# Weight casts moved to later rounds, x loaded first, and the second block's gates ahead of the first up projection, in a hybrid decoder layer on eight cores

## The chip, the cores and the metric

The kernel runs on the 8 cores of one Trainium2 chip. Each core computes one element of a batch of 8, and the cores exchange nothing. The metric is device time in microseconds (us) of the slowest core. Most executions of one kernel agree within 0.3%. In some executions the cores of one die, or of both, show a lower granted TensorE clock (0.80 to 0.95 instead of about 0.97) and the time is longer. Such slow runs are in no comparison below.

## The reference, cut to what matters

```python
# x: (8, 4096, 1024) f32; D = 1024, one layer
z = h @ w_in                        # -> q | k | v (768 each), u (512), g (2048)
# B: dilated causal window attention, 3 groups (window, dilation) x 4 heads of 64,
#    the groups mixed by their softmax denominators -> y_attn (4096, 256)
# A: s5_ssm(u): 32 groups of 16 channels, 64 complex states, a scan over 4096 steps
y_ssm = gelu(s5_ssm(u, ...)); a, b = split(y_ssm @ w_glu); y_ssm = a * sigmoid(b)
gate_ssm, gate_attn = split(sigmoid(g + b_gate))
mix = (gate_ssm * (y_ssm @ w_ssm_proj) + gate_attn * (y_attn @ w_attn_proj)) @ w_out
h = layer_norm(ALPHA * h + mix)
ff = square(relu(h @ w_up)) @ w_down           # 1024 -> 4096 -> 1024
h = layer_norm(ALPHA * h + ff)
```

## The kernel before

Every operation is recorded with the resources that it reads and writes. A list scheduler (I call it the planner) with constant cost estimates then fixes the order of every engine's instructions. The engines run these orders strictly in sequence and wait on semaphores. The planner's times are no times of the chip.

The stages of one core:

1. Load x and the first weights; U, the state-space layer's input projection (TensorE); "prep", its tables (VectorE, GpSimd).
2. Six rounds (three dilations, two head pairs). Each computes q, k and v of its heads and then attends. The state-space layer's 32 groups run in between.
3. Eight blocks of 512 tokens: gates g (GLU, gates, branch projections), o (output projection, first layer norm), up, d (down, second layer norm). Block b's gates are computed after up of block b-1, and its o inside d of block b-1.

Weights lie in DRAM as f32. Matmuls read bf16 copies (`wb_*`) made by casting transfers, here called casts. In rounds 1 and 2 there are 18 casts, 16 of 512 KB and two (`wb_ap`) of 256 KB, counted in bytes written; up and down are cast on the way to SBUF in block 0 (`first`) and stored from there for the later blocks.

```python
# loads at the start
dma("pool", wu[0].ap, wu_d[0], [], [wu[0]])
for s in range(8):
    dma("pool", xT.ap[:, :, s * 512:(s + 1) * 512], xT_d[s], [], [xT.res[s]])
    if s == 0:
        ...                                  # the other wu, then wq of round 0
...
dma("sp", smI.ap, smI_d, [], [smI])          # tables of the state-space layer
dma("sp", smB.ap, smB_d, [], [smB])

# U: two buffers us, stored to u_d
for fp in range(2):
    for s in range(8):
        for ft in (2 * fp, 2 * fp + 1):
            ub = us[ft % 2]
            ...                              # 8 matmuls
            cp("act", ub.ap[:, :, s * 32:(s + 1) * 32], ..., [bk], [ub])
    for ft in (2 * fp, 2 * fp + 1):
        dma("sp", u_d[ft], us[ft % 2].ap, [us[ft % 2]], [u_res.res[ft]])

# casts: a list of closures; each reads `pace`, the resource that it waits for
wcast.append(lambda pace, c=c_: dma("pool", dst[i, c], src[i, c]..., pace, [...]))
for name in ("glu", "gate", "sp", "ap", "out"):
    ...
# inside the rounds, after the copy of q or k (of v likewise)
cp("act", o, i, [bk], wr)
if rnd > 0 and t % 2 == 1 and wcast:
    wcast.pop(0)(wr[:1])       # the cast "reads" a part of qT or kT

# state-space layer: two store buffers
ysg = ysb[g % 2]
cp("act", ysg.ap, bk.ap..., [bk], [ysg])
for t in range(2):
    dma("act", y_d[g, :, t * 8:t * 8 + 8]..., ysg.ap[:, t, :], [ysg], [...])

# blocks: a ring of eight 1-MB slots for weights
def load_piece(name, i, first=False):
    slot = min((r for r in ring if id(r) not in live), key=last_use)
    if first:                                # cast into the slot, store bf16 for later
        dma("pool", slot.ap[:, 0:sz], src[i]..., [], [slot])
        dma("sp", dst[i], slot.ap[:, 0:sz], [slot], ...)
    else:
        dma("sp", slot.ap[:, 0:sz], dst[i], ..., [slot])

stage_g(0); ...                              # then stage_o of block 0
for blk in range(NB):
    stage_up(blk)                            # load_piece("up", up, blk == 0)
    if nxt:
        stage_g(blk + 1)
    pcs = [load_piece("dn", q, blk == 0) for q in range(4)]
    ...                                      # stage_d, with stage_o of the next block
```

The softmax here doesn't subtract the row's maximum and nothing guards it: scores larger than these inputs give would overflow.

## Time and profile before

The time is 2053.69 us (median of 6 runs, 2050.78 to 2062.69). The slowest core of the profiled run is core 3, and lines below without another core are of core 3.

From the page: the span, and three of the rows of 40 slices of about 51 us. A digit is the share of a slice in tenths that TensorE was busy, the granted TensorE clock, or the share that the core's 16 DMA engines were busy.

```profile
span 2049.2 us, 31367 instructions; the slowest of 8 cores (2035.1 to 2049.2 us)
...
PE   2898876999977697999999999999999999999996
...
PEclk8999988999998898999999999999999999999998
DMA  9946887551179949974565547366456543734531
```

Counting slices from 1, TensorE is full from slice 17 on; the change can only win before. The DMA row there shows 8, 8 and 7 in slices 5 to 7 (rounds 1 and 2, with the casts), 1 1 in slices 10 and 11 (rounds 4 and 5) and 9 9 in slices 13 and 14 (block 0). That is the invitation of this change: DMA work crowds where TensorE has gaps, and hardly any runs in rounds 4 and 5, where TensorE is full.

Waits of before (engine and line, what it waited for: us in total, times, longest):

```profile
ACT arena L497 <- DMA y_scratch<-arena: 16.8, 3, 11.4
...
ACT arena L497 <- DMA wb_out<-w_out: 16.0, 2, 9.4
...
PE ps L451 <- DMA arena<-wb_out: 9.3, 1, 9.3
...
PE ps L451 <- DMA arena<-w_down: 7.4, 1, 7.4
...
ACT arena L497 <- DMA wb_ap<-w_attn_proj: 5.7, 1, 5.7
```

The second and fifth line are the casts: ScalarE (ACT) copies into a part of qT, kT or V which a cast still "reads" as its pace token, and so waits until the cast has landed. This read is a fiction of the bookkeeping. The first line is different: the state-space output waits for a free store buffer, hence for a store that is slow in landing.

### The profile page before, as it was taken

What the parts mean: (1) busy time and instruction counts of PE and PEld (TensorE: products, weight loads), DVE (VectorE), ACT (ScalarE), POOL (GpSimd) and SP (SyncE); (2) the same over time, 40 slices, a digit from 0 to 9 for tenths busy, and PEclk for the clock granted to TensorE, in tenths of its full rate; (3) what the DMA queues carried; (4) which work ended last, traced back from release to release, by engine and by line L of the source; (5) the groups of instructions that cost most, each with busy time, mean ns of one, the idle gap of its engine ahead of it and who ended that gap; (6) DMA issues with size and microseconds to landing.
All of it is one profiled execution on the core that took longest, in us unless ns stands there. A gap on an engine that the chain in (4) does not pass through costs nothing.

```text
span 2049.2 us, 31367 instructions; the slowest of 8 cores (2035.1 to 2049.2 us)
## 1 busy us (share of the span) xinstructions
PE 1872.7 (91%) x10468; PEld 923.6 (45%) x10468; DVE 959.1 (47%) x1396; ACT 695.8 (34%) x1053; POOL 295.7 (14%) x322
## 2 busy tenths in 40 slices
PE   2898876999977697999999999999999999999996
PEld 1454453665643343444444444444444444444442
DVE  6944542763344431553553354256355336535524
ACT  2446432655564341224213213412421331232120
POOL 5743212120003002000100200100010020010000
PEclk8999988999998898999999999999999999999998
DMA  9946887551179949974565547366456543734531
GB/s 173 213 149 208 176 163 177 146 149 42 32 229 224 242 142 200 265 269 144 170 245 177 170 150 251 124 229 234 131 166 231 192 165 139 252 139 146 220 107 41
DMA packets 110189, 359.72 MB, mean 176 GB/s; under 512 B 10288, under 2 KB 55728, under 8 KB 81328
## 3 DMA queue, kind: packets, MB, share of 16 engines
q1 hardware_dynamic: 75872, 265.33, 37.8%
q0 software_dynamic: 25456, 83.99, 20.3%
q10 hardware_dynamic: 8704, 8.39, 1.3%
q8 instruction: 88, 1.44, 0.3%
q14 instruction: 69, 0.57, 0.1%
HBM read 339.94 MB, written 74.97 MB: 202 GB/s over the span
## 4 chain that ended last, share of the span: by engine, by line
PE 73%; DVE 7%; DMA 7%; ACT 5%; issue 5%; POOL 1%; ACTq 1%; DVEq 0%; POOLq 0%; SPq 0%
PE ps L451 72%; DVE arena L491 4%; ACT arena L497 3%; DMA y_scratch<-arena 2%; ACT arena L463 2%; DVE arena L481 2%; DMA arena<-wb_out 1%; PE ps L456 1%; DMA wb_out<-w_out 1%; DMA arena<-x_tile 1%; ACT L463 1%; ACTq L441 1%; DVE arena L1084 1%; DMA tab_scratch<-arena 1%; POOL arena L481 0%
## 5 line engine op out<-in xcount | busy, mean ns | idle before, releaser
L451 PE MATMUL ps<-arena 128*128 128x512 bf16 (+4 forms) x10148 | 1854.7, 344 | 118.8 <-ACT arena L497 29.1
L451 PEld LDWEIGHTS ps<-arena 128*128 128x128 bf16 (+2 forms) x10148 | 908.5, 104 | 1046.0 <-issue 208.9
L463 ACT ACTIVATE arena<-ps 128x512 f32<-128x512 f32 (+2 forms) x384 | 261.2, 680 | 388.5 <-PE ps L451 301.9
L491 DVE SCALAR_TENSOR_TENSOR arena<-ps,arena 128x512 bf16<-128x512 f32 x256 | 176.8, 691 | 245.6 <-ACT arena L463 245.6
L481 DVE TENSOR_TENSOR arena<-arena 128x512 f32<-128x512 f32 (+7 forms) x267 | 195.3, 756 | 177.6 <-ACT arena L463 164.5
L481 POOL TENSOR_TENSOR arena<-arena 128x512 bf16<-128x512 f32 (+1 forms) x128 | 165.3, 1294 | 766.1 <-DVE arena L481 633.6
L481 DVE TENSOR_TENSOR arena<-ps,arena 128x512 f32<-128x512 f32 (+1 forms) x193 | 127.5, 687 | 290.4 <-PE ps L451 237.8
L463 ACT ACTIVATE arena<-arena 128x512 f32<-128x512 f32 (+6 forms) x186 | 101.5, 548 | 292.4 <-DVE arena L1086 256.8
L491 DVE SCALAR_TENSOR_TENSOR arena<-arena,ps 128x512 f32<-128x512 f32 x128 | 87.1, 686 | 228.3 <-PE ps L451 227.1
L497 ACT CAST arena<-ps 128x512 bf16<-128x512 f32 (+1 forms) x217 | 122.1, 569 | 180.9 <-PE ps L451 120.7
L491 DVE SCALAR_TENSOR_TENSOR arena<-arena 128x1024 f32<-128x1024 f32 (+1 forms) x131 | 167.1, 1276 | 21.2 <-ACT arena L463 6.5
L463 ACT ACTIVATE arena<-ps,arena 128x512 f32<-128x512 f32 x128 | 86.0, 687 | 165.6 <-POOL arena L481 138.7
L441 POOL DMA_DIRECT2D out<-arena x32 | 17.3, 541 | 597.8 <-DVE arena L491 597.8
L463 ACT ACT_TABLE_LOAD x42 | 53.9, 1283 | 143.7 <-DVE arena L1086 125.6
L1084 DVE BATCH_NORM_STATS2 arena<-arena 128x6 f32<-128x512 f32 x128 | 88.8, 694 | 12.2
L456 PE MATMUL ps<-arena 128*128 128x128 bf16 (+1 forms) x320 | 39.6, 243 | 40.7 <-ACT arena L497 21.4
L497 ACT COPY arena<-ps 128x512 f32<-128x512 f32 (+1 forms) x64 | 51.2, 799 | 65.1 <-PE ps L456 27.2
L497 ACT CAST arena<-arena 128x1024 bf16<-128x1024 f32 x32 | 33.5, 1046 | 103.2 <-DVE arena L491 103.2
L456 PEld LDWEIGHTS ps<-arena 128*128 128x128 bf16 (+1 forms) x320 | 29.1, 122 | 62.1 <-issue 61.8
L481 DVE TENSOR_TENSOR arena<-arena,ps 128x512 f32<-128x512 f32 x64 | 41.0, 681 | 7.8 <-PE ps L451 7.8
L487 POOL TENSOR_SCALAR arena<-arena 128x256 f32<-128x256 f32 x32 | 39.1, 1224 | 9.4 <-DMA tab_scratch<-arena 6.4
L488 DVE TENSOR_SCALAR arena<-arena 128x512 f32<-128x512 f32 (+2 forms) x19 | 9.5, 498 | 43.7 <-POOL arena L487 43.3
(28 smaller groups left out, 153.6 us busy)
## 6 DMA issues: line engine op xcount, KB each, us to landing
arena<-wb_up SPq DMA_DIRECT2D x56, 1024.0 KB, 9.7
arena<-wb_dn SPq DMA_DIRECT2D x56, 1024.0 KB, 4.9
arena<-wb_gate SPq DMA_DIRECT2D x32, 1024.0 KB, 6.2
arena<-wb_out SPq DMA_DIRECT2D x16, 1024.0 KB, 9.0
arena<-x POOLq DMA_DIRECT2D x32, 512.0 KB, 10.5
out<-arena POOLq DMA_DIRECT2D x32, 512.0 KB, 4.3
arena<-x_tile POOLq DMA_DIRECT2D x8, 1024.0 KB, 48.5
tab_scratch<-arena SPq DMA_DIRECT2D x16, 512.0 KB, 4.2
```

The source lines that it names most:

```text
L441: return P.add(eng, lambda e: e.dma_start(out=out, in_=in_), R(*reads), R(*writes), dma=True, nbytes=nb)
L451: return P.add("pe", lambda e: e.matmul(out, lhsT, rhs, start=start, stop=stop, **kw), R(*reads), R(*writes), cost=c)
L456: return P.add("pe", lambda e: e.transpose(out, in_, ident), R(*reads), R(*writes), cost=c)
L463: return P.add("act", lambda e: e.activation(out, in_, func, bias=bias, scale=scale), R(*reads), R(*writes), cost=c, aset=ASETS.get(func))
L481: return P.add(eng, lambda e: e.tensor_tensor(out, in0, in1, op), R(*reads), R(*writes), cost=ew_cost(eng, out, [in0, in1], True))
L487: return P.add(eng, lambda e: e.tensor_scalar(out, in0, s1, None, op0), R(*reads), R(*writes), cost=c)
L488: return P.add(eng, lambda e: e.tensor_scalar(out, in0, s1, s2, op0, op1), R(*reads), R(*writes), cost=c)
L491: return P.add("dve", lambda e: e.scalar_tensor_tensor(out, in0, scalar, in1, op0, op1), R(*reads), R(*writes), cost=160.0 + 1.06 * fsize( ...
L497: return P.add("act", lambda e: e.copy(out, in_), R(*reads), R(*writes), cost=c)
L1084: P.add("dve", (lambda hf_: lambda e: e.bn_stats(st6[:, hf_ * 6:hf_ * 6 + 6], xb.ap[:, hf_ * 512:hf_ * 512 + 512]))(hf), R(xb), R(m), cost ...
```

## The change

Its intent: take the casts out of the crowded rounds 1 and 2 and put them, with the 16 casts of the down weights, into rounds 3 to 5; give x the first DMA time; let block 0 start without waiting for the attention's buffers; fill TensorE's gaps in block 0 with block 1's gates.

```diff
-    dma("pool", wu[0].ap, ...); for s in range(8): x tile s, after tile 0 the other weights
+    for item in ("u0", 0, "u1", "q0", "q1", 1, "q2", 2, "u2", "u3", 3, 4, 5, 6, 7):
+        ...                                     # numbers are x tiles
-    dma("sp", smI.ap, smI_d, [], [smI])
+    dma("sp", smI.ap, smI_d, [xT.res[XS]], [smI])          # XS = 2; smB likewise
-    dma("pool", shf.ap, shf_d, [], [shf])
+    dma("pool", shf.ap, shf_d, [xT.res[7]], [shf])
...
-    for name in ("glu", "gate", "sp", "ap", "out"):
+    for name in ("glu", "gate", "sp", "ap", "out", "dn"):
...
+    def pace(op, rnd, t):
+        if rnd > 2 and t % 2 == 1 and wcast:
+            after = Res()
+            after.w = op                        # waits for the copy, blocks nobody
+            wcast.pop(0)([after])
-                cp("act", o, i, [bk], wr)
-                if rnd > 0 and t % 2 == 1 and wcast:
-                    wcast.pop(0)(wr[:1])
+                pace(cp("act", o, i, [bk], wr), rnd, t)      # of v likewise
...
-            dma("sp", ya_d[...], ys_.ap, ...)
+            dma("act", ya_d[...], ys_.ap, ...)
...
+    ar.seek(E0, S1)                             # the state-space layer's region
+    ring = [ar.alloc([4096], BF16)]             # first slot; then yf, xTb, yT
     ar.seek(X0, Q0)
-    ring = [ar.alloc([4096], BF16) for _ in range(8)]
+    ring += [ar.alloc([4096], BF16) for _ in range(7)]      # mixin here; lnr, hT moved too
...
+            P.at("p3", 3)                       # the output projection's add goes first
             stt(xo, xo, ALPHA, bk.ap, ALU.mult, ALU.add, [x_, bk], [x_])
...
+    load_x(1)
+    stage_g(1)
     for blk in range(NB):
         stage_up(blk)
-        if nxt:
+        if nxt and blk:
             stage_g(blk + 1)
-        pcs = [load_piece("dn", q, blk == 0) for q in range(4)]
+        pcs = [load_piece("dn", q) for q in range(4)]        # the other four likewise
```

More of the change, by code (lines that the diff above doesn't have):

```diff
@@ L24 @@
 KB = 1024
+XS = 2
 class Res:
@@ L558, in build_program @@
     P.at("U", 2)
-    dma("pool", wu[0].ap, wu_d[0], [], [wu[0]])
-    for s in range(8):
-        dma("pool", xT.ap[:, :, s * 512:(s + 1) * 512], xT_d[s], [], [xT.res[s]])
-        if s == 0:
-            for ft in range(1, 4):
-                dma("pool", wu[ft].ap, wu_d[ft], [], [wu[ft]])
-            for j in range(3):
-                dma("pool", wq[j].ap, wqkv_d[0, :, j * 8:(j + 1) * 8, :], [], [wq[j]])
+    for item in ("u0", 0, "u1", "q0", "q1", 1, "q2", 2, "u2", "u3", 3, 4, 5, 6, 7):
+        if isinstance(item, int):
+            dma("pool", xT.ap[:, :, item * 512:(item + 1) * 512], xT_d[item], [], [xT.res[item]])
+        elif item[0] == "u":
+            dma("pool", wu[int(item[1])].ap, wu_d[int(item[1])], [], [wu[int(item[1])]])
+        else:
+            j = int(item[1])
+            dma("pool", wq[j].ap, wqkv_d[0, :, j * 8:(j + 1) * 8, :], [], [wq[j]])
     n = 0
@@ L583, in build_program @@
     smI = ar.alloc([SI_N], F32)
-    dma("sp", smI.ap, smI_d, [], [smI])
+    dma("sp", smI.ap, smI_d, [xT.res[XS]], [smI])
     smB = ar.alloc([SB_N], F32)
-    dma("sp", smB.ap, smB_d, [], [smB])
+    dma("sp", smB.ap, smB_d, [xT.res[XS]], [smB])
     shf = ar.alloc([384], BF16)
-    dma("pool", shf.ap, shf_d, [], [shf])
+    dma("pool", shf.ap, shf_d, [xT.res[7]], [shf])
     gcs = [ar.alloc([2, 2, 256], F32) for _ in range(3)]
@@ L898, in build_program @@
             o = V.ap[:, t4 * 4:t4 * 4 + 4].rearrange("p b (s d) -> p b s d", d=64)[:, :, 0:3:2, :]
-            cp("act", o, bk.ap.rearrange("p (b s d) -> p b s d", b=4, s=2), [bk], [V.res[t4 * 4 + j] for j in range(4)])
-            if rnd > 0 and t4 % 2 == 1 and wcast:
-                wcast.pop(0)(V.res[t4 * 4:t4 * 4 + 1])
+            pace(cp("act", o, bk.ap.rearrange("p (b s d) -> p b s d", b=4, s=2), [bk],
+                    [V.res[t4 * 4 + j] for j in range(4)]), rnd, t4)
         if rnd < 5:
@@ L974, in norm @@
             tt("dve", ys_.ap[64:128], a1[64:128], rn.ap[64:128], ALU.mult, r1 + [rn], [ys_])
-            dma("sp", ya_d[hp, :, 2 * b:2 * b + 2, :].rearrange("p r c -> p (r c)"), ys_.ap, [ys_], [ya_res.res[hp * 8 + b]])
+            dma("act", ya_d[hp, :, 2 * b:2 * b + 2, :].rearrange("p r c -> p (r c)"), ys_.ap, [ys_], [ya_res.res[hp * 8 + b]])
         def pv(q, j, pt):
@@ L1011, in build_program @@
         c([])
-    ar.seek(X0, Q0)
-    ring = [ar.alloc([4096], BF16) for _ in range(8)]
-    ar.seek(Q0, Q1)
+    ar.seek(E0, S1)
+    ring = [ar.alloc([4096], BF16)]
+    yf = ar.alloc([4, 512], F32, nres=4)
     xTb = ar.alloc([8, 512], BF16)
     yT = ar.alloc([4, 512], BF16)
+    ar.seek(X0, Q0)
+    ring += [ar.alloc([4096], BF16) for _ in range(7)]
+    mixin = ar.alloc([8, 512], BF16, nres=8)
+    ar.seek(Q0, Q1)
     y2T = ar.alloc([4, 512], BF16, nres=4)
@@ L1020, in build_program @@
     gsb, gab = ar.alloc([512], F32), ar.alloc([512], F32)
-    ar.seek(E0, S1)
-    yf = ar.alloc([4, 512], F32, nres=4)
-    mixin = ar.alloc([8, 512], BF16, nres=8)
-    E1 = ar.off
+    lnr = [ar.alloc([D], F32) for _ in range(4)]
     ar.seek(Q1, A0)
@@ L1028, in build_program @@
     aT = ar.alloc([32, 512], BF16, nres=32)
-    ar.seek(E1)
+    ar.seek(S1)
     hT = ar.alloc([8, 512], BF16, nres=4)
-    lnr = [ar.alloc([D], F32) for _ in range(4)]
     hb = [ar.alloc([1024], BF16) for _ in range(1)]
@@ L1168, in stage_o @@
             xo = x_.ap[:, oh * 512:(oh + 1) * 512]
+            P.at("p3", 3)
             stt(xo, xo, ALPHA, bk.ap, ALU.mult, ALU.add, [x_, bk], [x_])
+            P.at("p3", 7)
         P.at("ln1", 4)
@@ L1217, in build_program @@
     done(*wo)
+    load_x(1)
+    stage_g(1)
     for blk in range(NB):
         nxt = blk + 1 < NB
-        if nxt:
+        if nxt and blk:
             load_x(blk + 1)
         stage_up(blk)
-        if nxt:
+        if nxt and blk:
             stage_g(blk + 1)
         P.at("p3", 7)
-        pcs = [load_piece("dn", q, blk == 0) for q in range(4)]
+        pcs = [load_piece("dn", q) for q in range(4)]
         if nxt:
             wo = [load_piece("out", oh) for oh in range(2)]
-        pcs2 = [load_piece("dn", 4 + q, blk == 0) for q in range(2)]
+        pcs2 = [load_piece("dn", 4 + q) for q in range(2)]
         for t in range(TB):
@@ L1237, in build_program @@
             done(*wo)
-        pcs2 += [load_piece("dn", 6 + q, blk == 0) for q in range(2)]
+        pcs2 += [load_piece("dn", 6 + q) for q in range(2)]
         for t in range(TB):
```

## The prediction

> **What bounds the kernel now.** TensorE: busy 1872.7 of 2049.2 us, 73% of the chain of waits. From 834 us on it is solid (the windows show 1177 of the last 1199 us busy; one 512-token block takes 172 us). The 176 us without a matmul lie almost all before 834 us: 48 in 0-125, 20 in 200-300, 16 in 300-350, 38 in 575-690, 18 in 690-850. Around them the granted clock falls too (0.59 in 675-700), as the Trainium skill, "TensorE: Matmul & The Clock Gate", Part 1, says of an idle array; a removed gap is worth more than its idle time.
>
> **Step 1, casts to rounds 3-5, with their own pace token.** In round 2 a cast reads part of qT or kT that a later copy writes again, so ACT waits for the cast's landing: 5.74, 6.55 and 9.42 us in the timeline; the chain has 6.6, 8.2 and 12.1 us of DMA there. The token removes this: about -20. In round 1 the state-space output stores wait behind casts (chain: 15.1 and 27.2 us of y_scratch stores, DMA share 0.8-1.0): about -20. But 34 casts instead of 18, each about 3.9 us of all 16 DMA engines (estimate: queue 0's busy share in 200-300), come to some 130 us inside rounds 3-5 (384 to about 560 us). Round 3 still holds the state-space work until 460, so y_scratch waits return in part: +15. "DMA: Bandwidth & Descriptors", Issuing engines are not separate DMA queues: all queues share these engines, so moving work helps only where they were free (0.17 in 475-575). Net -22.
>
> **Step 2, x first.** Now x tile 0 lands at 20.4 us, tile 7 at 92. Moving tables and weights behind brings tiles 0-2 some 5-8 us earlier, but tile 7 no earlier: same bytes. The prep chain on VectorE/GpSimd (97 and 84 of 125 us busy) starts at 10 us now, and would wait for tile 2, about 40-46 us. Prep would end near 150 instead of 125, about when TensorE finishes U and q/k/v of round 0. Net 0, between -8 and +12.
>
> **Step 3, end of attention and first blocks.** First buffers outside the attention's region, attention stores on ACT: glu load and gelu come before 574; -5. Block 1's gates (about 45 us of matmul) fill the layer-norm gaps of 657-691 (16 of 34 us busy): -18. Down weights already bf16: the waits of 7.4 us for w_down and 9.3 for wb_out vanish, first down group and cold clock together -22. Against it, the up casts (wait to landing 9 to 35 us) now get ring slots only as block 1's gates release them: +10. Net -35.
>
> Steady blocks stay.
>
> **Sum:** 2053.7 - 22 - 0 - 35 = about 1997 us, range 1968 to 2030. Faster by over 2% (below 2012.6): 0.75; within 2%: 0.22; slower: 0.03.
>
> **What would show it.** Step 1: ACT no longer waits for wb_ap/wb_out casts; DMA share low in 200-350 and 0.8 or more in 400-560; rounds 1 and 2 about 40 us shorter together (the q/k/v weight loads mark them). Step 2: tile 1 lands before 32 us, table small loads issue near 40 us, attention of round 0 starts within 12 us of 186. Step 3: no TensorE wait for w_down; TensorE over 85% busy from the first glu to the first down group, and that stretch (574 to 822 us, 248 us) about 35 us shorter; blocks still 172 us.
>
> **What would make it wrong.** Prep so delayed that state-space and attention start 20 us late; casts so dense in rounds 3-5 that stores, weights or GpSimd's in-order queue stall TensorE; a first up starved by its casts.

## More of the kernel before

Windows of before, core 3 (window, its length, busy us of PE, PEld, DVE, ACT and POOL with instructions in brackets, granted clock, DMA share, GB/s):

```profile
190.00:345.00 155.00, 118.39 (x902) 70.33 (x902) 70.58 (x113) 58.11 (x83) 31.77 (x37) 0.87 0.82 167
345.00:445.00 100.00, 93.28 (x852) 61.47 (x853) 61.89 (x95) 59.30 (x94) 22.87 (x19) 0.97 0.61 169
445.00:565.00 120.00, 118.32 (x1111) 74.60 (x1109) 47.34 (x74) 63.81 (x92) 5.78 (x8) 1.00 0.19 43
565.00:665.00 100.00, 77.90 (x442) 37.64 (x441) 42.66 (x67) 57.01 (x72) 20.28 (x26) 0.88 0.83 230
665.00:860.00 195.00, 160.17 (x745) 72.06 (x743) 76.45 (x112) 56.73 (x80) 16.07 (x19) 0.89 0.84 202
```

Where TensorE has gaps (118 of 155 us busy), its granted clock is lower as well (0.87). Where it is full the clock is 1.00. The Trainium skill, "TensorE: Matmul & The Clock Gate", Part 1, describes a throttle that activity releases. The trace agrees.

DMA issues of before (engine queue, count, KB each, median us from issue to landing):

```profile
wb_gate<-w_gate POOLq DMA_DIRECT2D x8, 512.0 KB, 10.3
...
wb_out<-w_out POOLq DMA_DIRECT2D x4, 512.0 KB, 9.7
```

## The result, and the profile after

| | median us | range of all runs | runs |
|---|---|---|---|
| before, run beside after | 2054.08 | 2049.3 to 2293.99 | 40 |
| after | 2032.82 | 2027.23 to 2257.8 | 20 |

The ratio is 0.9892, 95% interval 0.9882 to 0.9901: 1.1% faster, within 2%. A ratio here is the mean time of one kernel's fast runs over that of the kernel before in the same rounds, so not quite the ratio of the medians. The prediction said 1997 us and a range of 1968 to 2030; the median is about 3 us above its end. The profiled run of after is a fast one. The slowest core is core 2; of its page:

```profile
span 2032.8 us, 31184 instructions; the slowest of 8 cores (2010.4 to 2032.8 us)
PE 1853.8 (91%) x10298; PEld 922.5 (45%) x10468; DVE 960.4 (47%) x1396; ACT 697.7 (34%) x1053; POOL 299.3 (15%) x330
...
PE   4878999769958799999999999999999999999996
...
PEclk8999999889979899999999999999999999999998
DMA  9858557789985799363574456366456553734621
```

TensorE's busy time is 19 us lower than before's 1872.7, but this is no saved work: 10298 matmul records stand beside 10468 weight loads, so 170 records are missing (core 3, whose records are complete, has 1867.1 us). Weight loads, 10468 in both traces, are the safer ruler. The rows tell the outline. The DMA digits of slices 5 and 6 went from 8 8 to 5 5, those of slices 10 and 11 from 1 1 to 9 9, as planned. TensorE gained in slices 1, 5 to 7, 13, 14 and 16, and lost in 3, 8, 9 and 12.

Windows of after, core 3 (columns as above):

```profile
190.00:345.00 155.00, 147.45 (x1345) 96.74 (x1343) 97.31 (x149) 86.24 (x126) 35.51 (x32) 1.00 0.61 166
345.00:445.00 100.00, 75.71 (x602) 47.38 (x601) 44.19 (x70) 43.95 (x70) 20.03 (x24) 0.85 0.77 148
445.00:565.00 120.00, 114.67 (x1058) 72.39 (x1056) 41.59 (x67) 66.48 (x92) 15.69 (x31) 0.97 1.02 138
565.00:665.00 100.00, 59.68 (x298) 25.94 (x296) 34.55 (x54) 44.17 (x56) 13.12 (x13) 0.78 0.70 209
665.00:860.00 195.00, 189.04 (x900) 85.25 (x901) 97.79 (x144) 62.70 (x90) 18.69 (x24) 0.98 0.74 202
```

The first window (rounds 1 and 2) went from 118 to 147 us busy at clock 1.00 instead of 0.87, the last (block 0) from 160 to 189. In between, where the casts went, it fell from 93 to 76, and around the end of the attention from 78 to 60 of 100 us, at a clock of 0.78. The DMA share of 445 to 565 us is 1.02 (shares over 1 occur in before too, up to 1.13 in its first 75 us, so packet times overlap in this view; read it as full).

To place the whole 2,030 us, I matched the weight-load records of each core, in their order, to the order of matmuls that the program issues, and read off where each stage ends. The table gives the mean of the eight cores of each profiled run, so its sums are not the slowest core's time. A round's column ends with its last q/k/v matmul. The attention of round 5 runs on into the column "then to o0" (to 624 us in before, 662 in after), which I call the end of the attention. "o0" is the first output projection and "up1" the first up matmul of block 1. Runs e1 to e18 are told below. For e1 to e4 the trace kept now is a second execution, whose stages differ from these rows by up to 3.6 us; read differences of a few us with that in mind.

| run (ratio) | to end of q/k/v of round 0 | rounds 1-2 | rounds 3-5 | then to o0 | o0 to up1 | rest | end |
|---|---|---|---|---|---|---|---|
| before | 175.4 | 203.3 | 189.9 | 82.3 | 230.8 | 1162.4 | 2044.1 |
| after (0.9892) | 190.6 | 155.4 | 221.5 | 96.5 | 195.8 | 1161.4 | 2021.2 |
| e1 old start (0.9954) | 175.8 | 160.9 | 246.3 | 94.3 | 195.9 | 1161.1 | 2034.3 |
| e2 token only (0.9970) | 176.3 | 195.3 | 192.8 | 81.6 | 232.6 | 1162.7 | 2041.3 |
| e3 planner only (0.9898) | 191.9 | 155.6 | 224.6 | 88.8 | 205.1 | 1161.2 | 2027.2 |
| e4 no down casts (0.9928) | 191.8 | 155.5 | 208.6 | 70.8 | 235.3 | 1160.9 | 2022.9 |
| e5 spread rounds 1-4 (0.9848) | 192.1 | 171.2 | 211.5 | 70.6 | 202.6 | 1161.4 | 2009.4 |
| e6 no deferral (0.9950) | 176.3 | 160.6 | 248.0 | 93.3 | 196.7 | 1161.1 | 2036.0 |
| e7 gates late (1.0066) | 191.8 | 155.5 | 225.8 | 97.8 | 227.1 | 1161.7 | 2059.7 |
| e8 rounds 2-4 (0.9972) | 192.1 | 171.3 | 219.9 | 92.7 | 202.5 | 1161.3 | 2039.8 |
| e9 18 casts, old place (0.9929) | 192.4 | 176.2 | 191.0 | 70.9 | 236.6 | 1161.2 | 2028.3 |
| e10 y in bf16 (0.9822) | 192.0 | 156.0 | 214.1 | 94.6 | 197.0 | 1161.5 | 2015.2 |
| e13 start only (0.9961) | 190.0 | 180.7 | 189.5 | 82.6 | 231.3 | 1162.7 | 2036.8 |
| e14 no down casts, gates late (0.9794) | 190.1 | 155.6 | 208.0 | 70.9 | 214.7 | 1160.9 | 2000.2 |
| e15 e5 and y in bf16 (0.9768) | 190.7 | 173.8 | 200.5 | 71.2 | 197.9 | 1161.4 | 1995.5 |
| e16 e14 and y in bf16 (0.9773) | 190.4 | 155.8 | 203.4 | 70.7 | 215.0 | 1161.1 | 1996.4 |

From before to after: +15.2, -47.9, +31.6, +14.2, -35.0 and -1.0 us. About 83 us were won in two stretches, as predicted, and 61 were given back in three.

The waits of after, core 3, that answer to those of before (L452, L464, L482 and L498 are before's L451, L463, L481 and L497):

```profile
PE ps L452 <- ACT arena L464: 41.6, 16, 18.7
...
DVE arena L482 <- DMA ya_scratch<-arena: 22.7, 2, 13.8
...
ACT L464 <- DMA arena<-y_scratch: 12.8, 1, 12.8
ACT arena L498 <- DMA y_scratch<-arena: 11.7, 2, 9.8
```

No wait for a cast remains, and none for w_down. There are new waits at the end of the attention. Their chain in the timeline of after, core 3 (start, duration, engine, what it did; in brackets idle time before it and what ended that):

```profile
555.99 0.33 ACTq L442 DMA_DIRECT2D ya_scratch<-arena  x1
...
581.52 0.32 SPq L442 DMA_DIRECT2D arena<-ya_scratch  x1
581.54 1.48 DVE L482 TENSOR_TENSOR arena<-arena 64x512 bf16<-64x512 f32 x2 [8.86 <-DMA ya_scratch<-arena]
581.99 1.74 SPq L442 DMA_DIRECT2D arena<-y_scratch  x4
...
588.03 1.28 ACT L464 ACT_TABLE_LOAD   x1 [12.83 <-DMA arena<-y_scratch]
...
593.51 0.51 PE L452 MATMUL ps<-arena 64*128 64x256 bf16 x4 [18.67 <-ACT arena L464]
```

The same store, and the load that waits for it, in before:

```profile
562.26 0.32 SPq L441 DMA_DIRECT2D ya_scratch<-arena  x1
564.09 0.32 SPq L441 DMA_DIRECT2D arena<-ya_scratch  x1
```

Read it as a relay. The 128-KB store at 555.99 is the first of the second head pair. Two things wait for it: the load of block 0's attention output, and VectorE, whose next result but one goes into the same buffer. Both move at 581.5, so the store took about 25.5 us to land. (In before the load follows the store by under 2 us.) The y load stands behind that load in SyncE's queue. It lets ScalarE do the gelu, ScalarE's exponentials of the attention stand behind the gelu in its queue, and TensorE waits for them 18.7 us. Why stores land late is seen in the issues of after (core 2, the slowest; on core 3 wb_dn takes 20.9 us and wb_out 18.6):

```profile
wb_dn<-w_down POOLq DMA_DIRECT2D x16, 512.0 KB, 23.6
...
wb_gate<-w_gate POOLq DMA_DIRECT2D x8, 512.0 KB, 11.6
...
wb_out<-w_out POOLq DMA_DIRECT2D x4, 512.0 KB, 22.4
```

wb_out takes 22.4 us from issue to landing instead of 9.7: casts are issued faster than the DMA engines carry them away, and the store of the relay waits beside them.

Late landings are not all of it. The order in which the planner puts TensorE's instructions comes out when the kernels are built. In after, the last 52 attention matmuls stand in one piece behind all of block 0's gates; in e4, e5 and e14 they alternate with gates. A window of after, core 3, at that piece (no wait of TensorE in it ends with a DMA):

```profile
636.00:664.00 28.00, 9.29 (x57) 4.01 (x56) 13.42 (x21) 13.31 (x19) 3.97 (x6) 0.59 0.78 233
```

The five kernels with this piece (after, e1, e6, e7, e10) take 93 to 98 us at the end of the attention. The eight that alternate (e4, e5, e9, e14 to e18) take 70 to 72, among them e14, whose wb_out takes 16.9 us to land on core 3. So the late store and the order share these 25 us. Only e3 below, where the piece is broken up and the late store stays, separates them in part.

### The profile page after: what moved, and what is told of

Same layout as the page of the kernel before. It is cut to its first block, busy times and chain, and to the rows that moved or that the text cites. A ratio compares the mean times of both kernels' runs of the same rounds, so it can differ in the third digit from the quotient of the medians.

```text
span 2032.8 us, 31184 instructions; the slowest of 8 cores (2010.4 to 2032.8 us)
## 1 busy us (share of the span) xinstructions
PE 1853.8 (91%) x10298; PEld 922.5 (45%) x10468; DVE 960.4 (47%) x1396; ACT 697.7 (34%) x1053; POOL 299.3 (15%) x330
## 4 chain that ended last, share of the span: by engine, by line
PE 70%; DMA 9%; DVE 6%; issue 6%; ACT 5%; ACTq 2%; POOL 1%; DVEq 0%; another core or an unknown queue 0%; SPq 0%; POOLq 0%
PE ps L452 69%; DVE arena L492 4%; ACT arena L464 2%; DMA arena<-x_tile 2%; DVE arena L482 2%; ACT arena L498 2%; DMA wb_up<-arena 2%; DMA y_scratch<-arena 2%; ACTq L442 2%; DMA ya_scratch<-arena 1%; PE ps L457 1%; DMA arena<-wb_out 1%; ACT L464 1%; DMA arena<-w_up 1%; DMA tab_scratch<-arena 0%
## 5 line engine op out<-in xcount | busy, mean ns | idle before, releaser
L452 PE MATMUL ps<-arena 128*128 128x512 bf16 (+5 forms) x9978 | 1837.1, 343 | 142.9 <-ACT arena L464 46.7
L452 PEld LDWEIGHTS ps<-arena 128*128 128x128 bf16 (+1 forms) x10148 | 908.2, 103 | 1052.8 <-issue 217.6
L464 ACT ACTIVATE arena<-ps 128x512 f32<-128x512 f32 (+2 forms) x384 | 261.5, 681 | 408.9 <-PE ps L452 293.0
L482 DVE TENSOR_TENSOR arena<-arena 128x512 f32<-128x512 f32 (+7 forms) x267 | 198.8, 769 | 235.6 <-ACT arena L464 191.1
L482 POOL TENSOR_TENSOR arena<-arena 128x512 bf16<-128x512 f32 (+1 forms) x128 | 164.7, 1291 | 673.2 <-DVE arena L482 525.7
L482 DVE TENSOR_TENSOR arena<-ps,arena 128x512 f32<-128x512 f32 (+1 forms) x193 | 127.4, 687 | 270.0 <-PE ps L452 201.8
L464 ACT ACTIVATE arena<-arena 128x512 f32<-128x512 f32 (+6 forms) x186 | 101.3, 546 | 288.7 <-DVE arena L1090 249.8
L498 ACT CAST arena<-ps 128x512 bf16<-128x512 f32 (+1 forms) x217 | 121.4, 569 | 161.7 <-PE ps L452 122.5
L464 ACT ACTIVATE arena<-ps,arena 128x512 f32<-128x512 f32 x128 | 86.0, 686 | 163.1 <-POOL arena L482 144.3
L498 ACT COPY arena<-ps 128x512 f32<-128x512 f32 (+1 forms) x64 | 51.1, 799 | 59.8 <-PE ps L457 27.0
L498 ACT CAST arena<-arena 128x1024 bf16<-128x1024 f32 x32 | 33.4, 1045 | 99.8 <-DVE arena L492 99.8
L457 PEld LDWEIGHTS ps<-arena 128*128 128x128 bf16 (+1 forms) x320 | 27.8, 118 | 39.8 <-issue 39.6
L482 DVE TENSOR_TENSOR arena<-arena,ps 128x512 f32<-128x512 f32 x64 | 40.9, 680 | 2.5 <-PE ps L452 2.5
L442 POOL DMA_DIRECT2D arena<-x x32 | 17.0, 534 | 98.4 <-DMA out<-arena 72.7
```

Of the source, the lines that this page charges most:

```text
L442: return P.add(eng, lambda e: e.dma_start(out=out, in_=in_), R(*reads), R(*writes), dma=True, nbytes=nb)
L452: return P.add("pe", lambda e: e.matmul(out, lhsT, rhs, start=start, stop=stop, **kw), R(*reads), R(*writes), cost=c)
L457: return P.add("pe", lambda e: e.transpose(out, in_, ident), R(*reads), R(*writes), cost=c)
L464: return P.add("act", lambda e: e.activation(out, in_, func, bias=bias, scale=scale), R(*reads), R(*writes), cost=c, aset=ASETS.get(func))
L482: return P.add(eng, lambda e: e.tensor_tensor(out, in0, in1, op), R(*reads), R(*writes), cost=ew_cost(eng, out, [in0, in1], True))
L498: return P.add("act", lambda e: e.copy(out, in_), R(*reads), R(*writes), cost=c)
```

## The experiments

All runs passed the comparison with the reference. Each expectation stands as it was written before the run; where it names a theory by a letter or calls it a rival, it says what that theory claims. Medians are of all runs of a kernel and can hold slow ones. Before's median in the groups of runs was 2051.6 to 2058.1; the groups ran on five chips, so compare ratios and not medians.

### Start of the kernel: e1, e6, e13

Round 0 ended 15 us later after the change. Theory: the new start costs these 15 us. Rival: it repays them, since U and prep end earlier. e1 is after with the old load order and tables at once, e6 is after with the new order and tables at once, and e13 is before with the new start alone.

```diff
# e1
-    for item in ("u0", 0, "u1", "q0", "q1", 1, "q2", 2, "u2", "u3", 3, 4, 5, 6, 7):
+    for item in ("u0", 0, "u1", "u2", "u3", "q0", "q1", "q2", 1, 2, 3, 4, 5, 6, 7):
# e1 and e6
-    dma("sp", smI.ap, smI_d, [xT.res[XS]], [smI])      # smB, shf likewise
+    dma("sp", smI.ap, smI_d, [], [smI])
# e13: before, with the first part of the diff of the change
```

> The changed kernel with the start undone (old load order, small tables at once). The changed kernel ends the q/k/v of round 0 at 191 us, 15 us later than before. Theory A (the deferred tables delay the prep and all that follows): round 0 ends near 176 again, and the total is 2033 - 15 = about 2018 us. Rival (TensorE has other work to catch up with, and rounds 1 and 2 were shortened by the new start rather than by the moved casts): total within 4 us of 2033, round 1 longer than 85 us.

> The changed kernel with its new load order but the small tables and shifts loaded at once. Undoing both cost 13 us. Theory B (U ends at 145 instead of 164 us, and the mask-free prep tail, which reuses U's store buffer, ends 17 us earlier, because with late tables the planner gives TensorE's early time to U): the deferral does it, so this kernel is like the one with the start undone, about 2046 us, U ending near 164. Rival (it is the tile order that brings tiles 1 and 2 sooner): about 2033, U ending near 145.

> The kernel before with only the new start (load order, deferred tables). Theory C (the start is worth something by itself: U ends near 145 instead of 164 us and the state-space layer begins at 170 instead of 183): 8 us or more faster than before, ratio 0.996 or less. Rival (its 13 us are only that the state-space layer, ending at 436 instead of 469, clears the way for the dense casts of rounds 3 to 5, which the kernel before has not): within 4 us of before.

Measured: e1 0.9954 (0.9907 to 1.0000), median 2046.22. Round 0 did end at 175.8, but the whole is some 13 us slower than after: both expectations missed, one had 15 us of gain and the other no change. e6: 0.9950 (0.9922 to 0.9978), 2046.15, so the deferral of the tables does it. The order of the loads is worth nothing with tables at once; beside the deferral it was not tested alone. e13: 0.9961 (0.9940 to 0.9983), with two fast runs only (2043.0 and 2045.4); its profiled run is 7 us shorter than before's in the table. The new start gains about 8 us alone and about 13 beside the rest.

The mechanism was not the one that I predicted. In before, prep ends at 181.6 us (mean of cores), since its last copies go into the buffers from which U is stored. Timeline of before, core 3:

```profile
164.45 2.37 SPq L441 DMA_DIRECT2D u_scratch<-arena  x2
...
174.15 1.29 DVE L498 CAST arena<-ps 128x512 bf16<-128x512 f32 x2 [0.33 <-DMA u_scratch<-arena]
```

The copy at 174.15 waits for the store issued at 164.45 (only 0.33 us, since other work stood before it in the fixed order). By the matched weight loads of core 3, 196 of prep's 216 are done by 126 us, and the last 20 come from 174 us on. In after the same stores go out some 20 us earlier:

```profile
142.30 0.38 SPq L442 DMA_DIRECT2D u_scratch<-arena  x1
...
146.41 0.37 SPq L442 DMA_DIRECT2D u_scratch<-arena  x1
```

With the tables held back, the planner has U to put first on TensorE, before q/k/v of round 0. Round 0's q/k/v end later, and U (163.8 to 144.8 us), prep (181.6 to 164.8) and the state-space layer's end (454.0 to 436.1) come earlier. In e1 and e6 the state-space layer runs until about 469, amid the casts, and rounds 3 to 5 take 246 and 248 us instead of 221.5. The growth is in rounds 4 and 5 (e6: 73.1 and 77.0 us, after: 63.4 and 61.2; round 3 97.9 and 96.8). For round 5, after the state-space layer, its cause is not shown.

### Pace token alone: e2

```diff
# before; of v likewise
-                    wcast.pop(0)(wr[:1])
+                    tok = Res()
+                    tok.w = P.all[-1]
+                    wcast.pop(0)([tok])
```

> The kernel before with nothing changed but the pace token of the casts. Theory A: ACT no longer waits for a cast's landing in round 2 (21.7 us of waits before), round 2 falls from 88 to about 70 us and the total by 17 to 22 us, to about 2034: as much as the whole change gave. Rival (the DMA engines are the limit there, the wait only moves to the state-space stores): the total falls by under 8 us.

Measured: 0.9970 (0.9947 to 0.9992), 2050.84. ScalarE's waits for casts are gone from the waits, and round 2 went from 91.5 to 81.8 us (78.3 in the second execution). But only about 6 us of the 20 that I had put down for the token arrived (2 to 11 by the interval). The casts still take DMA time in the same rounds; what the freed copies wait for next was not traced.

### The order at the end of the attention: e3, e12

Is the loss at the end of the attention an accident of order? e3 tells the planner that the attention's DMAs don't queue behind others, which changes the order there: the piece of 52 is broken up, though 66 gate matmuls now follow the attention, which is not the order of e4 either. e12 puts the attention's stores back on SyncE's queue.

```diff
# e3: in schedule(), after a DMA's end was estimated
+                if op.stream == "att":
+                    op.fin = t + issue + 3000.0
# e12
-            dma("act", ya_d[...], ys_.ap, ...)
+            dma("sp", ya_d[...], ys_.ap, ...)
```

> The changed kernel with only its static planner told that attention's own DMAs do not queue; same transfers, another order in the queues: the last attention units of round 5 come amid block 0's gates instead of behind them. Theory A (the order exposes the tail: 28 us of chained ACT and VectorE work with TensorE at 29 percent): total 2033 - 25 = about 2008 us. Rival (the down casts crowd the attention stores, 23 us to land, and hold the tail back whatever the order): within 8 us of 2033.

> The changed kernel with the attention stores issued from the sync queue again. Prediction's step 3 put 5 us on the earlier first loads. Theory A: the first gates start later, total +5. Rival (the store lands no sooner from either queue, since the engines are full; ACT saves its issue time): within 4 us of 2033.

Measured: e3 0.9898 (0.9879 to 0.9917), 2034.76, and e12 0.9895 (0.9877 to 0.9912), 2033.70, against after's 0.9892. Neither changes the whole. e3 won 7.7 us before the first output projection and lost 9.3 behind it. The late store is still there in e3 (issued at 565.84, its load at 586.42, core 3 of the kept trace), and 18 us of the 25.7 remain. So order alone does not explain them; no run has the casts of after with the order of e4. The Trainium skill, "DMA: Bandwidth & Descriptors", Issuing engines are not separate DMA queues, says that a DMA issued from another engine ends on the same 16 engines. e12 fits that: 0.0003 of ratio between the two queues.

### How much casting, and where: e4, e5, e8, e9

Theory: 34 casts do not fit in rounds 3 to 5. An estimate for one cast from before's trace: between 200 and 300 us the queue of casts and weight loads took the time of all 16 engines for 50 us, for about 12 casts and a few smaller weight loads, so about 3.9 us of all engines each. 34 of them are some 133 us. Rounds 3 to 5 of before lasted 190 us (379 to 569), of which other transfers already took some 63: 66 us at a share of 0.61 and 120 at 0.19, by the windows. That is 196 of 190 us. In after the stretch took 221 us, and the queues took 90% of it (core 3, 346 to 567 us: 72.6, 12.5 and 4.6%), some 198 us.

```diff
# e4 and e9: no down casts in the rounds, down through the ring as before
-    for name in ("glu", "gate", "sp", "ap", "out", "dn"):
+    for name in ("glu", "gate", "sp", "ap", "out"):
-        pcs = [load_piece("dn", q) for q in range(4)]
+        pcs = [load_piece("dn", q, blk == 0) for q in range(4)]      # and the others
# e9 also
-        if rnd > 2 and t % 2 == 1 and wcast:
+        if rnd > 0 and t % 2 == 1 and wcast:
# e5: 34 casts in rounds 1 to 4, nine a round
+        if rnd > 0 and t in (1, 4, 7) and wcast:
# e8: 34 casts in rounds 2 to 4, twelve a round as in after
+        if rnd > 1 and t % 2 == 1 and wcast:
```

> The changed kernel without the 16 down-weight casts in rounds 3 to 5; the down weights are cast through the ring in block 0 as before. Theory A: round 4 falls from 63.6 to about 57 us, the attention tail is no longer exposed (-25), the first down group again waits (+18): total about 2018 us; round 3 keeps most of its 98 us, since its 12 casts are the glu, gate and ssm ones. Rival (the down casts are harmless, the early start is what costs): the total rises by 15 to about 2048.

> The changed kernel with the same 34 casts paced three per eight copies over rounds 1 to 4 instead of four per eight over 3 to 5. Theory B (formed after the first four runs: what the casts cost is DMA time where the engines are already full; between 200 and 350 us the share is 0.59, between 450 and 580 it is 0.96): the end of round 5 comes 8 us or more before the changed kernel's 567, block 0's first output projection near 635 instead of 664 because the attention stores land in a few us again, total 2033 - 20 = about 2013 us. Rival (a cast beside the state-space stores costs as much as one beside the end of attention): rounds 1 and 2 grow by what the end gains, total within 6 us of 2033.

> The changed kernel with the same pace of casts (four per eight copies) one round earlier, rounds 2 to 4. Theory B: round 2 (77 us) and round 3 each hold state-space stores and grow as round 3 did, by about 20 us together beyond the changed kernel, while round 5 and the end of attention are free (-30): total about 2023. Rival (only the amount of casting counts, not the place): 2033 within 5.

> The changed kernel with the 18 old casts in rounds 1 and 2 where they were (but with the pace token) and the down weights cast in block 0: against the run without down casts (ratio 0.9928) only the place of the 18 casts differs. Theory B (a cast beside the state-space stores costs the same in rounds 1 and 2 as in 3): round 1 grows from 79 to about 105 us, round 3 falls from 96 to about 78, the total stays within 6 us of that run (2039). Theory A of the prediction (leaving rounds 1 and 2 is worth 20 us): about 2055.

| | ratio (95%) | median us |
|---|---|---|
| e4 | 0.9928 (0.9900 to 0.9956) | 2043.26 |
| e5 | 0.9848 (0.9827 to 0.9869) | 2025.62 |
| e8 | 0.9972 (0.9942 to 1.0002) | 2049.61 |
| e9 | 0.9929 (0.9907 to 0.9950) | 2043.29 |

- Without the down casts (e4) the rounds 3 to 5 shrink by 12.9 us and the end of the attention by 25.7, so the down casts cost 39 us there, the change of order included. But o0 to up1 grows by 39.5, since down now comes through the ring in block 0; the expectation had put 18 there, and so missed. The whole is slower than after by 0.4%, by the mean of cores by 1.7 us only: e4's cores end between 1999.7 and 2036.0.
- e9 against e4: with the 18 casts back in rounds 1 and 2, under the new token, the time is the same (0.9929 and 0.9928). Rounds 1 and 2 lose 20.7 us, rounds 3 to 5 win 17.6. Beside the other parts of the change, moving these 18 casts is worth nothing (within some 7 us, by the intervals).
- e5: the same 34 casts, spread over four rounds, gain 0.4% over after. The end of the attention takes 70.6 us instead of 96.5, and rounds 3 to 5 take 211.5. In the issues of e5 the median landing of wb_dn is 10.4 us and of wb_out 7.9 (after: 23.6 and 22.4). The DMA backlog is gone. The expectation (about 2013) was half met: round 5's q/k/v ended at 575 us and not before 559, since rounds 1 and 2 grew by 15.8.
- e8 missed: the expectation had a gain, and it is 0.8% slower than after. Its state-space layer ends at 489 us instead of 436. Rounds 1 and 2 grew by 15.9 us and the end of the attention fell by 3.8 only, to 92.7, although the DMA share there is low (0.30 and 0.45 from 565 to 600 and to 665 us, core 3). Its order differs: 124 attention matmuls are left when the last q/k/v matmul ends, against 84 in after. So twelve casts a round were worse earlier, beside more of the state-space layer, but how much of that is order is open.

### Gates early or late, down casts in the rounds or in block 0: e7, e14

These two complete a square with after and e4.

```diff
# e7 and e14: the gates of block 1 go back behind the first up
-    load_x(1)
-    stage_g(1)
-        if nxt and blk:
+        if nxt:
# e14: also e4's edit
```

> The changed kernel with block 1's gates after the first up again. Theory A: the layer-norm gaps of block 0 are open again; from the first output projection to the first down group grows by 15 to 20 us and the total to about 2050. Rival (the first up, fed by casts of its own, starves more when it comes later, so the early gates also buy or cost DMA time): total within 6 us of 2033.

> The changed kernel without the down casts and with block 1's gates late: the missing corner. The early gates are worth 36 us beside the down casts. Theory C (most of that is the hiding of damage by the down casts, which make the attention tail and with it the x loads of block 0 late): without down casts the early gates are worth 12 us or less, so this kernel is at 2051 or below, faster than the run with late gates and down casts (ratio 1.0066). Rival (the early gates fill the layer-norm gaps and are worth 30 us or more in either case): 2070.

| ratio (95%) | gates early | gates late |
|---|---|---|
| down casts in the rounds | after 0.9892 (0.9882 to 0.9901) | e7 1.0066 (1.0034 to 1.0098) |
| down casts in block 0 | e4 0.9928 (0.9900 to 0.9956) | e14 0.9794 (0.9768 to 0.9820) |

e7 has two fast runs (2067.1 and 2071.2), e14 a median of 2012.16. e7 lost about twice what was expected, and e14 is 39 us below the 2051 of its expectation. The two additions interact strongly. Beside the down casts in the rounds, early gates are worth 1.8% (1.0066 over 0.9892). Beside down casts in block 0 they cost 1.4% (0.9928 over 0.9794). And with neither the kernel is about 20 us faster than the whole change. (The means of cores, 2021.2, 2059.7, 2022.9 and 2000.2, give the same square.) The stage table says why. Against e14, e7's down casts cost 12 to 27 us in each of three places (rounds 3 to 5, up to o0, o0 to up1), and nothing fills the last. With gates early (after), that stretch is 195.8. In e4, on the other hand, the ring's casts come late. Windows of e14 and then of e4, core 3:

```profile
565.00:690.00 125.00, 98.49 (x476) 43.82 (x477) 64.04 (x95) 68.71 (x88) 19.54 (x25) 0.87 0.91 221
690.00:860.00 170.00, 169.04 (x805) 76.96 (x804) 78.39 (x115) 48.05 (x72) 19.29 (x25) 1.00 0.93 255
```

```profile
565.00:690.00 125.00, 97.48 (x469) 42.57 (x468) 59.83 (x89) 79.81 (x92) 19.35 (x22) 0.89 0.78 224
690.00:860.00 170.00, 138.71 (x639) 61.74 (x638) 60.99 (x90) 40.76 (x63) 15.16 (x20) 0.90 0.87 203
```

e14 has TensorE full from 690 us on, at clock 1.00 and beside a DMA share of 0.93. e4 loses 30 us of TensorE work there. The gates hold ring slots, so the casts of up start 67 us later. The same rows of the view of tile w_up, of e14 and then of e4 (issue min/median/max in ns, first and last start):

```profile
L442 POOL DMA_DIRECT2D arena<-w_up x8: 527/567/567, 581.1 to 638.6; - x8
```

```profile
L442 POOL DMA_DIRECT2D arena<-w_up x8: 527/567/567, 648.1 to 715.2; - x8
```

That e14 beats before's own block 0 so clearly (o0 to up1 214.7 against 230.8) has a likely cause, not tested alone: before's first w_down load came late. The whole difference lies between the first down matmul and up1 (92.1 us in before, 73.4 in e14). GpSimd's instructions of before and of e14, core 3:

```profile
761.42 1.27 POOL L481 TENSOR_TENSOR arena<-arena 128x512 bf16<-128x512 f32 x1 [89.53 <-DVE arena L481]
766.91 1.26 POOL L481 TENSOR_TENSOR arena<-arena 128x512 bf16<-128x512 f32 x1 [4.22 <-DVE arena L481]
768.12 1.63 POOL L441 DMA_DIRECT2D arena<-w_down  x3
```

```profile
716.92 0.53 POOL L442 DMA_DIRECT2D arena<-w_down  x1 [77.83 <-PE ps L452]
...
729.09 1.27 POOL L482 TENSOR_TENSOR arena<-arena 128x512 bf16<-128x512 f32 x1 [4.85 <-DVE arena L482]
```

Such a load casts, and the Trainium skill, "DMA: Bandwidth & Descriptors", SWDGE vs HWDGE vs iDMA, allows a cast only to DMAs issued from GpSimd. All w_down and `wb_*<-w_*` rows here are indeed POOL issues. In before this issue stood behind two adds of the gates in GpSimd's order, for which GpSimd waited 89.5 and 4.2 us; it came 51 us later than in e14. Which of the remaining parts of the change (buffers, priority of the add, load order) moved it is not settled.

### Two up pieces ahead of the gates: e18

If held ring slots are what makes e4 slow, loading two pieces of up before the gates take their slots should repair it.

```diff
# e4, and
+    P.at("p3", 7)
+    ups = [load_piece("up", u, True) for u in range(2)]
     load_x(1)
     stage_g(1)
-            piece = load_piece("up", up, blk == 0)
+            piece = ups[up] if blk == 0 and up < len(ups) else load_piece("up", up, blk == 0)
```

> The run with early gates and no down casts (ratio 0.9928), but the first two up pieces take their ring slots, and start their casts, ahead of block 1's gates. Theory D (the gates hold the ring and so hold back the casts, whose DMA time is missing later): the first two w_up casts start near 600 instead of 648 us, the first down group is 10 us or more shorter than 102 us, ratio 0.989 or less. Rival (the gates lack their slots in turn and TensorE waits for them instead): within 3 us of 0.9928.

Measured: 0.9879 (0.9863 to 0.9896), 2028.16, about 10 us better than e4. Its w_up row starts at 585.5 and ends at 699.0. But the stretch o0 to up1 shrank only to 231.1, still 16 us above e14, and the part of it from the first down matmul to up1 did not shrink (103.8 us; e4 102.1, e14 73.4). So the held slots are part of the cost. The rest I can only argue: with the gates gone from between up and down, no TensorE work is left there under which the down casts could land.

### Fewer bytes beside the casts: e10, e11, e15

If DMA time is the limit, halving the state-space output (y_scratch in bf16 instead of f32) should help, the most where it stores.

```diff
# e10: after; e11 and e15: e5
-    y_d = dram_tmp("y_scratch", [32, 16, 16, 256], F32)
+    y_d = dram_tmp("y_scratch", [32, 16, 16, 256], BF16)
-    ysb = [ar.alloc([2, 256], F32) for _ in range(2)]
+    ysb = [ar.alloc([2, 256], BF16) for _ in range(2)]      # e11: four buffers
-    yf = ar.alloc([4, 512], F32, nres=4)
+    yf = ar.alloc([4, 512], BF16, nres=4)
```

> The changed kernel with the state-space output stored as bf16 instead of f32: half the bytes of the stores that wait in round 3, the same number of transfers. Theory B (bytes on full engines): round 3 falls from 97 to about 88 us and the total by about 8, to 2025. Rival (the count of small packets or the landing time decides): round 3 within 3 us, total within 4 us of 2033.

> The spread casts (ratio 0.9848) together with the bf16 state-space output, four store buffers deep instead of two. Theory B: rounds 2 to 4 (91, 75 and 74 us there) shrink by about 15 us in all: total near 2010. Rival: within 4 us of 2023.

> The spread casts with the bf16 state-space output and the two store buffers as they were. If the two savings add (9 us of the spread, 14 us of bf16): ratio 0.978, about 2009 us. Rival (both free the same DMA time): as the run with four buffers, 0.981.

Measured: e10 0.9822 (0.9801 to 0.9843) with two fast runs, 2020.4 and 2018.2: 14 us of the slowest core. The mean of cores fell by 6.0 us only, as much as round 3 did (96.9 to 90.9), where the state-space layer ends among the casts. The rest is that the cores lie closer together (2012.0 to 2018.9; after 2010.4 to 2032.8), which is not explained. e11, with four store buffers, 0.9810 (0.9792 to 0.9829), 2018.21: between its two expectations; the planner's order changed with the buffers, and rounds 1 and 2 took 180.1 us instead of e5's 171.2. e15, the same with two buffers, 0.9768 (0.9747 to 0.9789), 2002.82: the lowest ratio of all and the first that is clearly faster by over 2%. The two savings add, as its expectation said.

### The other corner with fewer bytes: e16, e17

e16 is e14 with y in bf16. e17 also takes the 18 casts at six a round in rounds 2 to 4, to see whether their density in round 3 still costs.

```diff
# e16: e14 and the edit of e10; e17: e16 and
-        if rnd > 2 and t % 2 == 1 and wcast:
+        if rnd > 1 and t in (1, 5) and wcast:
```

> The best corner (no down casts in the rounds, block 1's gates late; ratio 0.9794) with the bf16 state-space output. Theory D (DMA time is what the first 850 us are short of): as in the changed kernel, where bf16 gave 14 us, about half of it in rounds 3 to 5: 7 us or more here, ratio 0.976 or less, about 2003 us. Rival (the corner is no longer held by DMA): within 3 us of 0.9794.

> The same with its 18 casts at half the pace, six a round in rounds 2 to 4. Theory D: round 3 (95 us with twelve casts) and round 4 fall by more than round 2 grows, since no stretch is then full: another 5 us or more, ratio about 0.973, round 3 below 88 us. Rival (the sum is what counts, not the pace): within 3 us of the run before it.

Measured: e16 0.9773 (0.9756 to 0.9789), 2006.18. bf16 gained 4 us here, against 14 in e10, and is not clear of the noise of e14; neither expectation (7 us or more, within 3) is decided. That the bytes of y compete with less beside 18 casts would fit, and is not shown. e17 0.9800 (0.9781 to 0.9818), 2014.52: in its profile round 2 takes 10.7 us more and round 3 9.3 less than in e16. Thinning 18 casts gained nothing: e17 is some 5 us above e16, with overlapping intervals. e15, e16 and e14 beat both kernels; their intervals overlap, so I do not rank them.

## Why the prediction was wrong

Predicted and measured by stretch (stage table, mean of cores, us):

| stretch | predicted | measured |
|---|---|---|
| to the end of round 0 (its q/k/v) | 0 | +15.2 |
| rounds 1 and 2 | -40 | -47.9 |
| rounds 3 to 5 | +15 | +31.6 |
| end of round 5 to o0 | -5 | +14.2 |
| o0 to up1 | -30 | -35.0 |
| rest | 0 | -1.0 |

(The terms of step 1 as written sum to -25, not to the -22 that it states; hence -60 here and -57 there.)

- **"What bounds the kernel now" held.** The steady blocks did not move (1162.4 and 1161.4), and removed gaps brought the clock up with them (0.87 to 1.00 in 190 to 345 us).
- **Step 1, "Net -22", is the step that failed.** The mechanisms were real: the waits for casts vanished and the DMA share in rounds 1 and 2 fell (0.82 to 0.61). The sizes were not. "The token removes this: about -20" is 6 by e2. Of the -47.9 in rounds 1 and 2 the new start alone brings 22.6 (e13), which leaves about -25 for the casts instead of -40, if the two add. "+15" for rounds 3 to 5 was +31.6. And +14.2 at the end of the attention was not foreseen at all. So step 1 came out near +20. The prediction itself counted some 130 us of cast time "inside rounds 3-5" and did not ask whether it fits beside what was there. It does not: the share reads 1.02, the later casts take 22 to 24 us to land, and a backlog runs on past the last round. At the end of the attention the planner's order, which the change altered, adds to it (e3: about 8 of 25 us, an estimate). Moving the 18 old casts is worth nothing (e9 against e4); the 16 down casts cost 39 us in these stretches (e4).
- **Step 2, "Net 0, between -8 and +12", was too cautious.** The start gained about 8 us alone (e13), the edge of the range, and 13 beside the rest (e1, e6), outside it. "Prep would end near 150 instead of 125" was right for most of prep (196 of 216 weight loads done by 126 us in before; by 155 in after) and missed its end: before's prep ended at 181.6, since its last copies hung on U's buffers. The prediction's test "attention of round 0 starts within 12 us of 186" looked at the wrong stage: the attention's first weight load came at 152 us (before: 163), the q/k/v of round 0 ended 15 us later, and the gain came in rounds 1 and 2, of whose -47.9 the start alone brings 22.6 (e13).
- **Step 3, "Net -35": the size for o0 to up1 about held (-35.0 for -30), the reading of it did not, so this agreement is partly luck.** The wait for w_down at the first down group vanished, as predicted. But the stretch that the prediction named, first glu to first down group, shrank by 14 us only (278.5 to 264.7, mean of cores), since it holds the end of the attention. And e14 has neither addition, and is 20 us faster than the kernel with both. Early gates and down casts in the rounds are each other's repair: together they save 19 us between o0 and up1 against e14 and cost 39 before it. The -5 for first buffers and stores on ACT: the store's queue is worth 0 (e12); the buffers were not tried alone.
- **"What would make it wrong"** named the right danger ("casts so dense in rounds 3-5 that stores, weights or GpSimd's in-order queue stall TensorE"), with too small a chance.

What stays open: the share of the moved buffers and of the add's priority, which were never run alone, why before's w_down load stood where it did in GpSimd's order, how the late stores and the planner's order share the end of the attention, and the rest of e18's loss.

## What to carry to other kernels

Before moving transfers into a quiet stretch, add up their DMA-engine time and what is there already: 133 us into 190 that held 63 filled the engines, and a small store that the next stage hung on then took 25 us instead of 2, so spreading (e5) or shrinking (e10) the bytes paid where moving them (e9) did not. Test two additions of one change as a square of four kernels: here each looked useful beside the other, and leaving both out was faster by 20 us. When a stage ends later, look at what ended earlier for it before undoing it. And where a planner fixes the order, compare the orders of two kernels before you put a difference down to the hardware.

## What the Trainium skill lacked or had wrong

- "DMA: Bandwidth & Descriptors", Anatomy of one DMA: its fit for DMAs issued from GpSimd, 2.0 us and bytes over 436e3, gives 3.2 us for the 512 KB that a cast writes, or 4.4 for the 1 MB of f32 that it reads (an estimate from this page). Here the median from issue to landing was 10.3 and 9.7 us in before (wb_gate, wb_out), 7.9 and 10.4 when spread (e5: wb_out, wb_dn), and 22.4 and 23.6 for the same two when twelve a round were issued (after). The page gives no landing time for a casting DRAM-to-DRAM transfer, nor for one among others that fill the engines; in engine time a cast took about 3.9 us of all 16 (an estimate from before's trace).
- No page says what casts do to the transfers beside them. Here a 128-KB store that landed in under 2 us in before took about 25.5 us in after, issued at a DMA share of 1.02.
- The same page, Issuing engines are not separate DMA queues, says that spreading DMAs over engines saves only issue time. It had it right (e12: 0.9895 against 0.9892), but that section doesn't warn that a DMA also waits for what stands before it on its issuing engine: before's w_down issue came directly behind an add at 766.91 us, for which GpSimd had waited; in e14 it went out 51 us earlier.
